# Loading the first branch's four attention arrays at once, two of them into a free tile of the split pool

## The chip, the cores and the metric

The kernel runs on one core of one Trainium2 chip. The metric is the device time of one execution in microseconds (us); lower is better. A core has five engines that run on their own and wait for each other through semaphores: TensorE (PE, matmuls), VectorE (DVE), ScalarE (ACT), GpSimd (POOL) and SyncE (SP). Here SP issues nearly all DMAs, POOL a few. A DMA that SP issues goes through a hardware queue, one that POOL issues through a software queue; both move their packets on the same 16 DMA engines.

## The reference

One decoder layer over 1024 tokens of width 1024, in f32. Two attentions run side by side, their outputs are projected, gated and added, and a feed-forward block follows. What matters here is the end of the mixer:

```python
oa, _ = banded_window_attention(qa, ka, va, A_WINDOW - 1, sinks)      # 16 heads of 64
ya = jnp.einsum('bte,ed->btd', oa.reshape(Bn, T, A_Q_W), w_branch_a)  # 1024 -> 1024
...
ob = jnp.sum(wts[..., None] * o_all, axis=0).astype(u.dtype)          # 8 heads of 64
yb = jnp.einsum('bte,ed->btd', ob.reshape(Bn, T, B_OUT_W), w_branch_b)
merged = jax.nn.sigmoid(ga) * ya + jax.nn.sigmoid(gb) * yb
return jnp.einsum('btd,de->bte', merged, w_o)
```

## The kernel before

Every f32 product is made of three fp32r matmuls (`mac`, L137 to L139): an operand is split into a rounded part `hi` and the rest `lo`, and hi·hi, hi·lo and lo·hi are summed in PSUM. Each operand must therefore be split before use: ACT copies it to `hi` and DVE subtracts to get `lo` (`split`, L117 and L118; for weights L78 and L79 in the class `Weights`).

In the first phase each pair of heads yields one array of attention output, 128x1024 f32 (512 KB). It is scaled and stored to DRAM: eight arrays `oa_d[0..7]` of the window attention, four `ob_d[0..3]` of the dilated one. The last of them, pair 7, is served by POOL instead of SP and DVE (`side`, L618): POOL stores the sums (L610), fetches them back spread over the partitions into the tile `vt` (L615, two DMAs of 256 KB), multiplies them into the tile `o` (L624) and stores `o` to `oa_d[7]` (L625).

The second phase projects them in three branches of four arrays each: branch 0 takes `oa_d[0..3]`, branch 1 `oa_d[4..7]`, branch 2 `ob_d`. A branch has eight steps (`dc`), each 24 matmuls for two PSUM tiles of 128x512. A step with dc = 0 runs with the array `k` as its outer loop: six matmuls for array 0, six for array 1, and so on. Before branch 0, PE multiplies one gate (48 matmuls, L137 to L139 on `u`), which needs none of the arrays.

`o_parts(b)` brings the four arrays of a branch in and splits them, in the order of `k`. `send_parts` issues the loads on SP. It has two raw tiles (`o_raw`, pool `mix`), so at most two arrays are on their way; each of the next two loads waits until a raw tile has been split. The results go into tiles `o_hl` of the pool `low`, six tiles of 8 KB per partition that are handed out in turn. When the second phase starts, the memory of `low` lies where tiles of the first phase were. A tile is free when the last instruction on the old tile in its place is done: the first tile of `low` has nothing to wait for, the second some stores of SP, the third the store of `o` by POOL, the fourth the two fetches into `vt`. SP, ACT, DVE and POOL each work strictly in the order in which the code issues.

The work of SP behind these loads, in order: weights of the branch (`w_raw`, L55), the columns of a modulation matrix (`a_raw`, L822).

Of the kernel before, what the change touches and what calls it, by code (L numbers as in the profile page):

```python
# [10 lines left out]
F32 = mybir.dt.float32  # L11
# [7 lines left out]
P = 128  # L19
T = 1024  # L20
# [78 lines left out]
def decoder_layer(ctx: ExitStack, tc: tile.TileContext, I, out, dbg=None):  # L99
# [685 lines left out]
    mix = ph2b.enter_context(tc.tile_pool(name="mix", bufs=2, reuse_waits="tile"))  # L785
# [7 lines left out]

    o_src = [oa_d[p] for p in range(A_PAIRS)] + [ob_d[p] for p in range(B_PAIRS)]
    o_raws, o_sent = [], [0]

    def send_parts(upto):
        while o_sent[0] < min(upto, len(o_src)) and len(o_raws) < 2:
            raw = mix.tile([P, T], F32, name="o_raw", bufs=2)
            nc.sync.dma_start(raw, o_src[o_sent[0]])  # L800
            o_raws.append(raw)
            o_sent[0] += 1

    def o_parts(b):
        parts = []
        for k in range(4):
            send_parts(4 * b + 4)
            hl = low.tile([P, 2, T], F32R, name="o_hl", tag="big")
            split(hl[:, 0], hl[:, 1], o_raws.pop(0))
            parts.append(hl)  # L810
        return parts
# [61 lines left out]
            nc.gpsimd.tensor_tensor(m, m, tmp, op=OP.add)  # L873

    mg = None
    send_parts(2)

    def split_merged(dcs):
        for dc in dcs:
# [5 lines left out]
    for kind, i in order:  # L885
        if kind == "g":
            if i in (8, 9, 17):
                ws.prepare(4)
                parts = o_parts({8: 0, 9: 1, 17: 2}[i])
                make_gate(i, ())  # L890
            else:
                make_gate(i)
            if i == 23:
                mg = wide("m", bigu)
                split_merged(range(0, 3))
            continue
        b, dc = steps[i]
        w = ws.take(1)
        ps = [ps_2.tile([P, TH], F32, name="p2") for _ in range(2)]
        for n, (t, k) in enumerate([(t, k) for t in range(2) for k in range(4)] if dc not in (0, KC - 1) else  # L900
                                   [(t, k) for k in range(4) for t in range(2)]):
            s = slice(t * TH, (t + 1) * TH)
            mac(ps[t], w(k), (parts[k][:, 0, s], parts[k][:, 1, s]), k == 0, k == 3)
            if n == 3:
                ws.step()
        if dc == 3:
            send_parts(len(o_src))
        for t in range(2):
            merge(b, dc, t, ps[t], gts.get(i))
        next(ada, None)  # L910
        if i == 22:
            split_merged(range(3, 6))
# [500 lines left out]
```

## Time and profile before

| | |
|---|---|
| median of three runs | 1901.1 us (1900.1 to 1901.41) |
| profiled execution, its own time | 1908.77 us |
| span of the profiled execution, first to last instruction | 1907.0 us |
| mean granted TensorE clock | 0.987 of full speed |
| PE busy | 1841.1 us, 97% of the span |
| PE waiting for the splits of branch 0 | 8.0 us in one wait, at 834.3 to 842.3 us |

Times inside the profile are us from the span's start. The profiled execution is 7.7 us longer than the median of the plain runs, and 1.8 us of it lie outside the span. A timeline names at each row the idle time ahead of it and what ended that.

### The profile page before, as it was taken

Reading aid. Unit: us, or ns where it says so; the run is one execution under the profiler, and the core shown is the slowest. Engines: PE = TensorE matmul, PEld = TensorE weight load, DVE = VectorE, ACT = ScalarE, POOL = GpSimd, SP = SyncE. Lnnn points to the kernel's source line nnn. Section 1 sums busy time; section 2 is a strip of 40 time slices with the busy share of each in tenths; the row PEclk is TensorE's granted clock in tenths of the full one; section 3 lists DMA queues with packets and bytes.
Section 4 is the critical chain, followed back from the end, with each engine's and each line's share of the span. In section 5 each row is a group of like instructions: output and inputs, shape, how many; then the busy total and the mean of one; then the engine's idle time right before and its main releaser. Section 6 shows DMA issues by size and latency. Waiting matters only on the chain.

```text
span 1907.0 us, 24471 instructions
## 1 busy us (share of the span) xinstructions
PE 1841.1 (97%) x8988; PEld 1489.6 (78%) x8988; DVE 1160.4 (61%) x2161; ACT 782.0 (41%) x1661; POOL 596.5 (31%) x389
## 2 busy tenths in 40 slices
PE   6899999999999999989999999999999999899998
PEld 5688877878878777768888878778888888788886
DVE  7855667667677887534555364575565444565557
ACT  3455545445444767633122132653333333412122
POOL 2432223223323222100311142455664333431213
PEclk9899999999999999989999999999999999999999
DMA  8011112111121122254534123123222222432222
GB/s 316 28 34 34 40 41 74 45 57 56 41 63 50 53 89 68 79 178 164 175 118 161 56 75 124 56 89 100 89 78 89 78 89 95 135 125 90 93 71 89
DMA packets 72266, 170.83 MB, mean 90 GB/s; under 512 B 13073, under 2 KB 14161, under 8 KB 72146
## 3 DMA queue, kind: packets, MB, share of 16 engines
q1 hardware_dynamic: 71810, 168.21, 26.7%
q8 instruction: 71, 1.16, 0.3%
q0 software_dynamic: 336, 1.06, 0.2%
q14 instruction: 49, 0.40, 0.1%
HBM read 145.80 MB, written 23.43 MB: 89 GB/s over the span
## 4 chain that ended last, share of the span: by engine, by line
PE 51%; DVE 3%; ACT 1%; issue 1%; DMA 1%; SPq 0%; POOL 0%; DVEq 0%; ACTq 0%; POOLq 0%
PE pf L1106 21%; PE p L138 5%; PE p L139 5%; PE p L137 5%; PE pf L137 5%; PE pf L139 5%; PE pf L138 5%; DVE m L118 1%; DMA h_raw<-h_d 0%; DVE wd L79 0%; DVE h L118 0%; DMA oa_d<-o 0%; PE px L1034 0%; PE p L835 0%; PE p L842 0%
## 5 line engine op out<-in xcount | busy, mean ns | idle before, releaser
L137 PE MATMUL pj<-u,w_hi 128*128 128x512 f32 x720 | 301.5, 419 | 0.0
L139 PE MATMUL pj<-u,w_lo 128*128 128x512 f32 x720 | 283.9, 394 | 0.0
L138 PE MATMUL pj<-u,w_hi 128*128 128x512 f32 x720 | 282.6, 392 | 0.0
L425 POOL TENSOR_TENSOR rb<-rb,sin_t 128x512 f32<-128x512 f32 x64 | 86.8, 1356 | 502.0 <-DVE rb L423 431.5
L118 DVE TENSOR_TENSOR w_lo<-r,w_hi 128x512 fp32r<-128x512 f32 x110 | 117.7, 1072 | 138.7 <-ACT w_hi L117 137.9
L79 DVE TENSOR_TENSOR w_lo<-w_raw,w_hi 128x512 fp32r<-128x512 f32 x150 | 133.4, 893 | 85.3 <-ACT w_hi L78 83.0
L528 ACT ACTIVATE probs<-probs,st 128x128 f32<-128x128 f32 (+1 forms) x320 | 146.0, 461 | 60.5 <-DVE st L518 30.8
L137 PEld LDWEIGHTS pj<-u,w_hi 128*128 128x128 f32 x720 | 136.4, 189 | 33.6 <-issue 4.7
L139 PEld LDWEIGHTS pj<-u,w_lo 128*128 128x128 f32 x720 | 135.8, 189 | 30.7
L138 PEld LDWEIGHTS pj<-u,w_hi 128*128 128x128 f32 x720 | 136.7, 190 | 22.6
L137 PE MATMUL pf<-wd,h 128*128 128x512 f32 x352 | 139.2, 395 | 3.4 <-DVE zt L1326 2.9
L138 PE MATMUL pf<-wd,h 128*128 128x512 f32 x352 | 138.7, 394 | 1.9 <-DVE wd L79 1.9
L139 PE MATMUL pf<-wd,h 128*128 128x512 f32 x352 | 138.6, 394 | 0.0
L62 POOL TENSOR_TENSOR w_raw<-w_raw,gate 128x512 f32<-128x512 f32 x60 | 83.1, 1404 | 157.0 <-DMA w_raw<-in_w_down 134.4
L1326 DVE SCALAR_TENSOR_TENSOR zt<-zt,pf 128x512 f32<-128x512 f32 x112 | 76.2, 685 | 85.1 <-PE pf L139 85.0
L426 POOL TENSOR_TENSOR r<-ra,rb 128x512 f32<-128x512 f32 x63 | 114.5, 1817 | 6.1 <-DVE kl L460 1.3
L78 ACT ACTIVATE w_hi<-w_raw 128x512 fp32r<-128x512 f32 x150 | 92.0, 624 | 29.0 <-PE p L138 12.0
L552 ACT ACTIVATE ptsb<-pt 128x512 f32<-128x512 f32 (+1 forms) x128 | 63.6, 548 | 93.6 <-PE pt L550 93.2
L137 PE MATMUL p<-u,w_hi 128*128 128x512 f32 x224 | 88.3, 394 | 0.0
L139 PE MATMUL p<-u,w_lo 128*128 128x512 f32 x224 | 87.2, 389 | 0.0
L138 PE MATMUL p<-u,w_hi 128*128 128x512 f32 x224 | 87.2, 389 | 0.0
L137 PE MATMUL p<-o_hl,w_hi 128*128 128x512 f32 x192 | 75.9, 395 | 8.0 <-ACT o_hl L117 8.0
(297 smaller groups left out, 4267.2 us busy)
## 6 DMA issues: line engine op xcount, KB each, us to landing
w_raw<-in_w_in SPq DMA_DIRECT2D x118, 256.0 KB
r<-in_w_gate_up SPq DMA_DIRECT2D x47, 512.0 KB
a_raw<-in_w_ada SPq DMA_DIRECT2D x32, 512.0 KB
w_raw<-in_w_down SPq DMA_DIRECT2D x44, 256.0 KB
h_raw<-h_d SPq DMA_DIRECT2D x22, 512.0 KB
h_d<-g SPq DMA_DIRECT2D x40, 256.0 KB
wa<-in_w_ada_m SPq DMA_DIRECT2D x16, 512.0 KB
wb<-wt_d SPq DMA_DIRECT2D x24, 256.0 KB
```

The source lines that it names most:

```text
L62: self.nc.gpsimd.tensor_tensor(self.raws[i], self.raws[i], scale(), op=OP.mult)
L78: self.nc.scalar.activation(hi, raw, AF.Copy)
L79: self.nc.vector.tensor_tensor(lo, raw, hi, op=OP.subtract)
L118: nc.vector.tensor_tensor(lo, src, hi, op=OP.subtract)
L137: nc.tensor.matmul(ps, w[0], m[0], start=first, stop=False)
L138: nc.tensor.matmul(ps, w[0], m[1], start=False, stop=False)
L139: nc.tensor.matmul(ps, w[1], m[0], start=False, stop=last)
L425: eng.tensor_tensor(b, b, sin_t[:, s], op=OP.mult)
L426: eng.tensor_tensor(residue_half(res, r, t), by_residue(a, r), by_residue(b, r), op=OP.add)
L528: nc.scalar.activation(pr, pr, AF.Exp, bias=st[:, 0, h, b:b + 1], accum_out=st[:, 1, h, b:b + 1])
L1106: nc.tensor.matmul(ps, w[:, c], m[:, k], start=first and k == 0 and n == 0, stop=k == 3 and n == 2, skip_group_check=True)
L1326: nc.vector.scalar_tensor_tensor(z, z, ALPHA if gi == 0 else 1.0, pd, op0=OP.mult, op1=OP.add)
```

## The change

The loads of branch 0's four arrays are issued together, ahead of the first split. Arrays 0 and 1 go into the two `o_raw` tiles as before. Arrays 2 and 3 go into `raw23`, a new tile with room for both, taken from the pool `low` ahead of the tiles for the splits. From the fifth array on the limit is two again.

```diff
     o_raws, o_sent = [], [0]
+    raw23 = low.tile([P, 2, T], F32, name="raw23", tag="big")
 
     def send_parts(upto):
-        while o_sent[0] < min(upto, len(o_src)) and len(o_raws) < 2:
-            raw = mix.tile([P, T], F32, name="o_raw", bufs=2)
+        while o_sent[0] < min(upto, len(o_src)) and len(o_raws) < (4 if o_sent[0] < 4 else 2):
+            raw = raw23[:, o_sent[0] - 2] if o_sent[0] in (2, 3) else mix.tile([P, T], F32, name="o_raw", bufs=2)
             nc.sync.dma_start(raw, o_src[o_sent[0]])
...
     mg = None
-    send_parts(2)
+    send_parts(4)
```

SP's queue where the second phase starts, before. The names in brackets are the semaphores that an instruction waits for: DMAHW0 to 7 stand for SP's own DMAs in turn, DVE, PE and Pool for those engines.

```order
L700 DMA ga_d_110<-r_7436 128x1024 [waits DMAHW7_49,DVE_49]
L800 DMA o_raw_7689<-oa_d_108 128x1024 [waits DMAHW0_49,PE_49]
L800 DMA o_raw_7691<-oa_d_108 128x1024 [waits DMAHW1_49,Pool_49]
L55 DMA w_raw_7697<-in_w_branch_a 128x512 [waits DVE_49]
L55 DMA w_raw_7703<-in_w_branch_a 128x512 [waits DMAHW3_49,DVE_49]
L800 DMA o_raw_7708<-oa_d_108 128x1024 [waits DMAHW4_49,DMAHW0_49,DVE_49]
L800 DMA o_raw_7713<-oa_d_108 128x1024 [waits DMAHW5_49,DMAHW1_49,DVE_49]
L822 DMA a_raw_7743<-in_w_ada 128x1024 [waits DMAHW6_49,PE_49]
L822 DMA a_raw_7771<-in_w_ada 128x1024 [waits DMAHW7_49]
```

The same place of SP's queue now:

```order
L700 DMA ga_d_110<-r_7436 128x1024 [waits DMAHW7_49,DVE_49]
L801 DMA o_raw_7690<-oa_d_108 128x1024 [waits DMAHW0_49,PE_49]
L801 DMA o_raw_7692<-oa_d_108 128x1024 [waits DMAHW1_49,Pool_49]
L801 DMA raw23_7688<-oa_d_108 128x1024
L801 DMA raw23_7688<-oa_d_108 128x1024 [waits DMAHW3_49]
L55 DMA w_raw_7700<-in_w_branch_a 128x512 [waits DMAHW4_49,DVE_49]
L55 DMA w_raw_7706<-in_w_branch_a 128x512 [waits DMAHW5_49,DVE_49]
L823 DMA a_raw_7742<-in_w_ada 128x1024 [waits DMAHW6_49,PE_49]
L823 DMA a_raw_7770<-in_w_ada 128x1024 [waits DMAHW7_49]
```

The loads of arrays 2 and 3 no longer wait for DVE's splits, stand ahead of the two weight loads, and nothing of the queue behind them waits for a split any more.

ACT's queue at the four splits of branch 0, before. DMASW3 is the semaphore of POOL's store of `o` to `oa_d[7]`, Pool that of POOL's product ahead of it, DMASW1 and DMASW2 those of POOL's two fetches into `vt`.

```order
L78 ACTIVATE w_hi_7699<-w_raw_7470 128x512 [waits DMAHW1_49]
L117 ACTIVATE o_hl_7705<-o_raw_7689 128x1024 [waits DMAHW0_49]
L117 ACTIVATE o_hl_7710<-o_raw_7691 128x1024 [waits DMAHW6_49,DMAHW1_49,DMAHW7_49,DVE_49,Activation_49]
L117 ACTIVATE o_hl_7715<-o_raw_7708 128x1024 [waits DMAHW4_49,DMASW3_49,Pool_49]
L117 ACTIVATE o_hl_7718<-o_raw_7713 128x1024 [waits DMAHW5_49,DMASW2_49,DMASW1_49]
L681 ACTIVATE gt_7721<-p2_7722 128x512 [waits PE_49]
```

The same four splits in ACT's queue now:

```order
L78 ACTIVATE w_hi_7702<-w_raw_7470 128x512 [waits DMAHW1_49]
L117 ACTIVATE o_hl_7708<-o_raw_7690 128x1024 [waits DMAHW6_49,DMAHW0_49,DMAHW7_49,DVE_49,Activation_49]
L117 ACTIVATE o_hl_7711<-o_raw_7692 128x1024 [waits DMAHW1_49,DMASW3_49,Pool_49]
L117 ACTIVATE o_hl_7714<-raw23_7688 128x1024 [waits DMAHW2_49,DMASW2_49,DMASW1_49]
L117 ACTIVATE o_hl_7717<-raw23_7688 128x1024 [waits DMAHW3_49]
L681 ACTIVATE gt_7720<-p2_7721 128x512 [waits PE_49]
```

`raw23` has the first tile of `low`, so each split has the tile after the one that it had: the waits for the old tiles stand one split earlier. The wait for POOL's store, at the third split before, is now at the second. DVE's four subtractions (L118) show the same shift. The order of the matmuls on PE and of all work on POOL is unchanged, and from branch 1 on every split waits as before.

## Rows read from the trace of the kernel before

**Rows 1.** The page's first part: busy time, share of the span and instructions of each engine.

```profile
PE 1841.1 (97%) x8988; PEld 1489.6 (78%) x8988; DVE 1160.4 (61%) x2161; ACT 782.0 (41%) x1661; POOL 596.5 (31%) x389
```

**Rows 2.** The waits of PE over the whole span: us in total, times, longest us.

```profile
PE pt L254 <- DVE acc L242: 11.4, 6, 7.8
PE p L137 <- ACT o_hl L117: 8.0, 1, 8.0
PE s L501 <- DVE qs L440: 7.2, 2, 6.4
```

**Rows 3.** The timeline of PE at the end of the gate and the first step of branch 0: start, us, instruction, and in brackets the idle time before it and what ended it.

```profile
830.58 0.39 PE L139 MATMUL p<-u,w_lo 128*128 128x512 f32 x1
830.80 0.39 PE L137 MATMUL p<-o_hl,w_hi 128*128 128x512 f32 x1
...
832.16 0.39 PE L137 MATMUL p<-o_hl,w_hi 128*128 128x512 f32 x1
832.90 0.50 PE L138 MATMUL p<-o_hl,w_hi 128*128 128x512 f32 x1 [0.35 <-DVE o_hl L118]
...
833.93 0.39 PE L139 MATMUL p<-o_hl,w_lo 128*128 128x512 f32 x1
842.32 0.80 PE L137 MATMUL p<-o_hl,w_hi 128*128 128x512 f32 x1 [8.00 <-ACT o_hl L117]
843.58 0.80 PE L138 MATMUL p<-o_hl,w_hi 128*128 128x512 f32 x1 [0.46 <-DVE o_hl L118]
...
844.60 0.63 PE L137 MATMUL p<-o_hl,w_hi 128*128 128x512 f32 x1
845.03 0.63 PE L138 MATMUL p<-o_hl,w_hi 128*128 128x512 f32 x1
```

**Rows 4.** The timeline of ACT from the first split to the second step of branch 0 and beyond; L866 empties a PSUM tile when its 12 matmuls are done.

```profile
827.82 1.06 ACT L117 ACTIVATE o_hl<-o_raw 128x1024 fp32r<-128x1024 f32 x1 [6.44 <-DMA o_raw<-oa_d]
830.53 1.06 ACT L117 ACTIVATE o_hl<-o_raw 128x1024 fp32r<-128x1024 f32 x1 [1.64 <-DMA o_raw<-oa_d]
841.21 2.00 ACT L117 ACTIVATE o_hl<-o_raw 128x1024 fp32r<-128x1024 f32 x2 [9.62 <-DMA oa_d<-o]
843.12 1.06 ACT L681 ACTIVATE gt<-p 128x512 f32<-128x512 f32 x2
844.08 0.63 ACT L78 ACTIVATE w_hi<-w_raw 128x512 fp32r<-128x512 f32 x1
...
854.08 0.60 ACT L866 ACTIVATE zt<-p 128x512 f32<-128x512 f32 x1 [2.12 <-PE p L139]
...
859.52 0.60 ACT L866 ACTIVATE zt<-p 128x512 f32<-128x512 f32 x1 [2.12 <-PE p L139]
```

**Rows 5.** The timeline of DVE at the same four splits.

```profile
828.92 1.23 DVE L118 TENSOR_TENSOR o_hl<-o_raw,o_hl 128x1024 fp32r<-128x1024 f32 x1 [6.73 <-ACT o_hl L117]
831.62 1.23 DVE L118 TENSOR_TENSOR o_hl<-o_raw,o_hl 128x1024 fp32r<-128x1024 f32 x1 [1.48 <-ACT o_hl L117]
842.30 2.36 DVE L118 TENSOR_TENSOR o_hl<-o_raw,o_hl 128x1024 fp32r<-128x1024 f32 x2 [9.46 <-ACT o_hl L117]
```

**Rows 6.** The timeline of POOL, all that it does between 821 and 904 us.

```profile
821.29 0.68 POOL L610 DMA_DIRECT2D wa_d<-sr  x1 [44.55 <-DVE sr L609]
825.34 1.03 POOL L615 DMA_DIRECT2D vt<-wa_d  x2 [3.36 <-DMA wa_d<-sr]
833.86 2.35 POOL L624 TENSOR_TENSOR o<-o,vt 128x1024 f32<-128x1024 f32 x1 [7.49 <-issue]
836.50 0.60 POOL L625 DMA_DIRECT2D oa_d<-o  x1 [0.30 <-POOL o L624]
```

**Rows 7.** The timeline of SP's DMA issues at the start of the second phase.

```profile
821.25 1.72 SPq L800 DMA_DIRECT2D o_raw<-oa_d  x2
823.02 0.90 SPq L55 DMA_DIRECT2D w_raw<-in_w_branch_a  x2
830.17 3.03 SPq L800 DMA_DIRECT2D o_raw<-oa_d  x2
833.29 0.86 SPq L822 DMA_DIRECT2D a_raw<-in_w_ada  x2
```

**Rows 8.** DMA traffic in two stretches, 826.5 to 833 us and then 831 to 834 us, by queue: packets, MB, share of the 16 engines (q1 is SP's queue, q0 POOL's); and the issues of POOL with the time from issue to landing.

```profile
q1 hardware_dynamic: 468, 1.15, 53.1%
q0 software_dynamic: 160, 0.52, 33.5%
...
q1 hardware_dynamic: 156, 0.57, 71.2%
...
oa_d<-o POOLq DMA_DIRECT2D x1, 512.0 KB, 4.6
```

**Rows 9.** Stretches of the trace: from and to in us, busy time of PE, PEld, DVE, ACT and POOL (instructions), granted TensorE clock, share of the DMA engines, GB/s.

```profile
674.20:677.60 3.40, 3.40 (x10) 2.77 (x10) 3.33 (x8) 1.97 (x5) 0.00 (x0) 0.51 0.64 158
...
826.40:827.80 1.40, 1.40 (x8) 1.17 (x7) 0.00 (x0) 0.00 (x0) 0.00 (x0) 1.00 1.02 389
827.80:830.40 2.60, 2.60 (x13) 2.13 (x13) 1.23 (x1) 1.06 (x1) 0.00 (x0) 1.00 0.97 241
830.40:832.60 2.20, 2.15 (x10) 1.46 (x8) 0.98 (x1) 1.06 (x1) 0.00 (x0) 1.00 0.70 203
...
842.30:848.30 6.00, 5.51 (x12) 4.08 (x13) 5.49 (x7) 3.00 (x5) 0.00 (x0) 0.50 0.08 22
```

## The prediction

> **What bounds the kernel now.** First the busy shares: PE is busy for 97% of the span, and no engine beside TensorE for more than 61% [rows 1]. So a change counts as far as it moves PE's idle time or its clock. Next the waits of PE, longest first: the second longest of all is a single wait of 8.0 us for ACT's split of an array of attention output [rows 2]. That is the place of the change. The timeline of PE shows where it lies: the gate's last matmul starts at 830.58, the six matmuls on array 0 from 830.80, the six on array 1 from 832.16 (with 0.35 us for DVE in between), and then nothing until 842.32, when array 2 is there [rows 3].
>
> Who ends that wait? The loads of arrays 2 and 3 were issued from 830.17, each when a raw tile had been split [rows 7], so it looks as if they came late because of that. The timeline of ACT says otherwise: the third split starts at 841.21, and the idle time before it is ended by the landing of POOL's store of `o` [rows 4]. That store was issued at 836.50 and took 4.6 us [rows 6, 8], which gives 841.1. Array 2 itself was long there: SP's queue moved 0.57 MB between 831 and 834 us, which is the whole of that load and a little more [rows 8]. The third split waits because its `o_hl` tile lies where POOL's `o` lay, as the order of ACT shows. The chain behind this wait is POOL's: sums stored at 821.29, fetched into `vt` from 825.34, product at 833.86 after 7.49 us of waiting for that fetch, store at 836.50 [rows 6].
>
> **What the change does, part by part.**
>
> *The loads.* Arrays 2 and 3 are issued about 7 and 9 us earlier, at about 823 to 825 us, and land before they are needed. By themselves they gain nothing, since the third split did not wait for its load. Arrays 0 and 1 are issued as before and ahead of them in the queue, so the first split starts at about 827.8 again. The two weight loads move back by the time of two issues, 1.7 us [rows 7]; they serve steps that begin after 850 us, and PE's time until then hides that. The two `a_raw` loads, which stood behind the waiting loads until 833.29, follow at about 826 us. Only DVE's sums of the modulation use them, behind the four splits in its queue, so they gain nothing either.
>
> *The wait that moves.* `raw23` takes the first tile of `low`, the one with nothing to wait for. The four splits have the second to fifth tile. The first split now waits for stores that SP issued before 821.25, ahead of its own load in the same queue: nothing. The second split now has the tile under POOL's `o`, and waits for the same store at 841.1 that the third waited for. So PE has the six matmuls of array 0 at 830.8, stops at 832.2 instead of 834.3, and resumes when the second split's first half is done, 1.06 us after the store lands [rows 4]: at 842.3 if the store is no later. The wait grows from 8.0 to about 10.1 us. Behind the second split on ACT stand the other two splits, the gate's two activations and the next weight split; they ran from 841.21 to 844.7 [rows 4] and take 1.0 us more with one more split ahead of them. On DVE it is 1.2 us more [rows 5]. The weights so delayed serve the third step, after 854 us, so nobody waits for that.
>
> *The price of it.* Before the change 12 of the step's 24 matmuls were left at 842.3, now 18. The six more cost, at full clock, a quarter of a step: successive steps end 5.44 us apart (854.08 to 859.52 [rows 4]), so **1.36 us**. At the lower clock, where matmuls start 0.43 us apart (844.60 to 845.03 [rows 3]), they would cost 2.6 us. I take 1.36, because what is at the lower clock is a stretch of time: PE resumes at 842.32 and runs at 0.50 of its clock until 848.3 [rows 9], and the six matmuls push the rest of the work to behind 848.3, where it runs at full clock. The other three splits cost nothing more: they follow each other on ACT at 1.0 us, and six matmuls take 1.4 us or more.
>
> *The store that may come later.* POOL's fetch into `vt` shares the DMA engines with SP's loads. Before, SP had little queued from about 828 to 831; now arrays 2 and 3 (1.05 MB), the weights and the `a_raw` loads (1.05 MB) stand there at once. No row shows the two queues full at the same time, so I bound the delay. From below: in the fetch's own stretch, 827.8 to 832.6, the engines moved 2.6 us at 241 and 2.2 us at 203 GB/s [rows 9], 1.07 MB, of which the fetch was 0.52 [rows 8]: it already shared about evenly. With even shares again it lands when it did, and the store might gain some tenths, since the `a_raw` loads that ran beside it are over: -0.3 us. From above: all of SP's loads go first. The traffic before, from 826.4 to 832.6, was 1.62 MB, some 0.35 of it from array 2; now 1.27 + 2.1 = 3.37 MB must move. With 0.52 MB at the fetch's pace (2.4 us at about 220 GB/s) and 2.85 MB at the 389 GB/s that SP's loads reached at 826.4 to 827.8 [rows 9] (7.3 us), that ends at 836.1 instead of 832.6: +3.5 us. I take **+1.0 us**, nearer to the even sharing, because that is what the one stretch with both queues shows, but not at it, since SP's queue now never runs dry.
>
> The Trainium skill (DMA: Bandwidth & Descriptors, Queues, rings and completion order) says that a DMA engine takes turns between the queues that have work, and changes only after a whole packet of descriptors. By that rule the fetch would wait for one packet of SP's at each turn and no longer, and the sum below would be near +1.4 rather than +2.4; the even shares in [rows 9] agree with it, and no row tests it with SP's queue full throughout.
>
> *The clock.* PE's stretch at 0.50 after the pause cost 3.0 us of full-clock work (half of 842.3 to 848.3 [rows 9]). The pause is now longer, but it was already long enough to lose the clock. Its end may come one short stretch earlier or later; the shortest low stretch here is 3.4 us, 674.2 to 677.6 [rows 9], worth 1.7 us. I take 0, and keep 1.7 both ways for the range.
>
> **The sum.** 1.36 + 1.0 = +2.4 us. The profiled execution was 1908.77 us with a span of 1907.0; after, about 1911.2 and 1909.4. It lies 7.7 us above the median of the plain runs; I carry the difference over to the median: 1901.1 + 2.4 = **1903.5 us**. PE works without a long break behind this place, so what it loses here it does not get back.
>
> **The rivals.**
>
> *The fetch is pushed far back (slower).* The same shift of the wait, but SP's loads go ahead of POOL's fetch nearly all the way: +1.36 + 3.5 = +4.9, 1906.0 us. It decides from a fetch that is 2.5 us later on, where the sum passes 3.8 us. For it: SP's queue holds 2.1 MB more in that stretch. Against it: the even sharing above, and that most of this traffic also ran before the fetch ended in the profile of before, array 2 beginning at 831.
>
> *The late loads were the cause (faster).* If the third split had waited for its load and POOL's store only landed at the same moment, the loads at once would end the stop: -8.0 us, and -3.0 us for the clock that is then not lost, 1890.1. For it: the loads did stand behind splits. Against it: the landing of array 2 by 834 [rows 8], and the wait for the store in ACT's order, which now stands at the second split.
>
> *Nothing changes.* The change doesn't do what it says to PE: the six matmuls fall into a stretch where something else holds PE up anyway, such as an earlier end of the low clock, 1901.1. For it: the sum is small. Against it: from 848.3 on PE runs without a gap that could hide it.
>
> **How the numbers follow.** Forecast 0.70; pushed-back fetch 0.20; late loads 0.04; nothing 0.06. A difference of 0.2% (3.8 us) is about what a measurement of this kernel can tell from no change, so the forecast at +2.4 and the case of no change count as the same, but for a tail of the forecast, 0.04, in which the delay and the clock both come out badly. That gives slower 0.20 + 0.04 = 0.24, same 0.66 + 0.06 = 0.72, faster 0.04. The range: down to no delay of the fetch and the clock back early, 1901.1 + 1.36 - 0.3 - 1.7 = 1900.5; up to the pushed-back fetch, 1906.0, and a little for the clock, 1906.4. This leaves out the late loads and the tails.
>
> **What would show it.** In the profile after: SP issues four loads in a row from 821.25 and the weights at about 825; ACT starts the first split at 827.8 and the other three in a row at about 842; PE's wait for ACT's split is about 10 to 11 us and begins at 832.2, after six matmuls and not twelve; POOL's product starts between 833.6 and 837.4, likely near 834.9. PE then runs some 6 us at half clock. I am wrong if the second split starts before POOL's store has landed, if the first split is late too, or if PE's wait is under 8 us.

## The result and the profile after

| | before | after |
|---|---|---|
| median of 20 runs of each | 1900.88 us (1899.09 to 1902.91) | 1903.53 us (1901.72 to 1905.84) |
| ratio after/before | | 1.0015 (95%: 1.0009 to 1.0021) |
| profiled execution | 1908.77 us | 1905.39 us |
| PE's wait for the splits of branch 0 | 8.0 us | 10.3 us |

The change makes the kernel 2.65 us slower by the medians (1.7 to 4.0 us by the interval of the ratio). That is 0.15%, clear of no change, and under the 0.2% that the prediction counted as a difference. The forecast was 1903.5.

Single profiles do not show that: the profiled execution of after is the shorter one. The profile of before held low-clock stretches far from this place, such as 674.2 to 677.6 us [rows 9], and its mean granted clock is 0.987, that of after 0.990. So the sum is made on the medians, and the place is read by itself. There, too, two traces are offset: TensorE's last transpose ahead of POOL's chain (L607) starts at 819.77 in before and at 818.06 in after. I call that start t0; "t0 + 7.18" is 7.18 us behind it, and all comparisons below are made so. Line numbers shift by one or two where an edit adds lines (L866 is L867 in after), and the profile leaves digits out of names, so `raw23` is `raw` there.

The waits of PE in after (us in total, times, longest):

```profile
PE pt L254 <- DVE acc L242: 11.9, 6, 7.1
PE p L137 <- ACT o_hl L117: 10.3, 1, 10.3
PE s L501 <- DVE qs L440: 7.2, 2, 6.4
```

The list is that of [rows 2], and one entry has moved by more than half a microsecond: 8.0 is now 10.3. PE's timeline in after, from the transpose at t0 to where it resumes:

```profile
818.06 0.27 PE L607 MATMUL pt<-ident,es 128*16 128x128 f32 x1
...
830.23 0.39 PE L139 MATMUL p<-o_hl,w_lo 128*128 128x512 f32 x1
840.95 0.80 PE L137 MATMUL p<-o_hl,w_hi 128*128 128x512 f32 x1 [10.34 <-ACT o_hl L117]
842.21 0.79 PE L138 MATMUL p<-o_hl,w_hi 128*128 128x512 f32 x1 [0.47 <-DVE o_hl L118]
```

PE stops after 830.6, at t0 + 12.6, when it has had the six matmuls of array 0. Before it stopped at t0 + 14.6, after twelve [rows 3]. It resumes at t0 + 22.89 (before t0 + 22.55). ACT's timeline says on what:

```profile
824.40 1.06 ACT L117 ACTIVATE o_hl<-o_raw 128x1024 fp32r<-128x1024 f32 x1 [4.72 <-DMA o_raw<-oa_d]
839.85 1.06 ACT L117 ACTIVATE o_hl<-o_raw 128x1024 fp32r<-128x1024 f32 x1 [14.38 <-DMA oa_d<-o]
840.81 1.99 ACT L117 ACTIVATE o_hl<-raw 128x1024 fp32r<-128x1024 f32 x2
...
848.28 1.28 ACT L867 ACTIVATE zt<-p 128x512 f32<-128x512 f32 x2 [3.99 <-PE p L139]
851.68 0.60 ACT L867 ACTIVATE zt<-p 128x512 f32<-128x512 f32 x1 [1.60 <-PE p L139]
854.40 0.60 ACT L867 ACTIVATE zt<-p 128x512 f32<-128x512 f32 x1 [2.12 <-PE p L139]
```

The second split, which reads a raw tile that landed long ago, waits 14.38 us for the landing of POOL's store `oa_d<-o`, as the third did before [rows 4]. The other two follow in a row. The fourth PSUM tile of the branch (the second half of the second step) is emptied at t0 + 36.34; before it was t0 + 34.31. POOL's timeline in after shows the chain behind the store:

```profile
819.59 0.68 POOL L610 DMA_DIRECT2D wa_d<-sr  x1 [44.55 <-DVE sr L609]
825.24 1.03 POOL L615 DMA_DIRECT2D vt<-wa_d  x2 [4.97 <-DMA wa_d<-sr]
834.19 2.33 POOL L624 TENSOR_TENSOR o<-o,vt 128x1024 f32<-128x1024 f32 x1 [7.92 <-issue]
836.82 0.60 POOL L625 DMA_DIRECT2D oa_d<-o  x1 [0.30 <-POOL o L624]
```

From t0 the fetch is issued at 7.18 (before 5.57), the product starts at 16.13 (14.09), the store is issued at 18.76 (16.73) [rows 6]. The DMA issues of POOL in after, with us from issue to landing:

```profile
oa_d<-o POOLq DMA_DIRECT2D x1, 512.0 KB, 3.0
vt<-wa_d POOLq DMA_DIRECT2D x2, 256.0 KB, 7.5
wa_d<-sr POOLq DMA_DIRECT2D x1, 8.0 KB, 5.1
```

The store is 2.03 us late, but lands in 3.0 us instead of 4.6 [rows 8], with nothing of SP's beside it any more: SP's queue moved 0.76 MB between 836.5 and 841.2 us in before and nothing between 836.82 and 839.85 us in after. So the second split is released at t0 + 21.79, only 0.35 us behind the third split of before. SP's issues in after are the four loads, the weights and the modulation's columns in one run:

```profile
819.54 1.42 SPq L801 DMA_DIRECT2D o_raw<-oa_d  x2
821.01 0.99 SPq L801 DMA_DIRECT2D raw<-oa_d  x2
822.10 0.96 SPq L55 DMA_DIRECT2D w_raw<-in_w_branch_a  x2
823.16 1.45 SPq L823 DMA_DIRECT2D a_raw<-in_w_ada  x2
```

All of them are issued when POOL's fetch is (825.24); before, half of them came after it [rows 7]. Two stretches of after: from the fetch's issue to the product, and PE's low clock once it resumes (columns as in [rows 9]):

```profile
825.24:834.19 8.95, 5.38 (x24) 4.13 (x22) 1.23 (x1) 0.22 (x1) 1.03 (x2) 0.99 1.03 332
...
840.95:847.70 6.75, 6.28 (x14) 4.62 (x15) 6.61 (x8) 3.33 (x5) 0.00 (x0) 0.50 0.04 5
```

The DMA engines are full over the 8.95 us from the fetch's issue to the product (share 1.03). PE runs 6.75 us at half clock after the pause (6.0 before [rows 9]).

### The profile page after: what moved, and what is told of

Read it like the earlier page. It is cut to its first block, busy times and chain, and to the rows that moved or that the text cites. A ratio compares the mean times of both kernels' runs of the same rounds, so it can differ in the third digit from the quotient of the medians.

```text
span 1903.6 us, 24471 instructions
## 1 busy us (share of the span) xinstructions
PE 1835.7 (96%) x8988; PEld 1484.8 (78%) x8988; DVE 1162.5 (61%) x2161; ACT 781.8 (41%) x1661; POOL 597.5 (31%) x389
## 5 line engine op out<-in xcount | busy, mean ns | idle before, releaser
L118 DVE TENSOR_TENSOR w_lo<-r,w_hi 128x512 fp32r<-128x512 f32 x110 | 117.7, 1073 | 138.7 <-ACT w_hi L117 136.6
L137 PE MATMUL p<-o_hl,w_hi 128*128 128x512 f32 x192 | 76.1, 396 | 10.3 <-ACT o_hl L117 10.3
```

The source lines that it names most:

```text
L118: nc.vector.tensor_tensor(lo, src, hi, op=OP.subtract)
L137: nc.tensor.matmul(ps, w[0], m[0], start=first, stop=False)
```

## The experiments

The theory on record for the first runs was the prediction's own: the wait for the old tile stands six matmuls earlier, and POOL's chain is a little later. The rival was that the loads at once are what costs, since they crowd POOL's fetch. Each run below is timed in turn with the kernel before on the same chip; a difference is that of the two medians (11 runs of each edited kernel that was timed, but 9 of e4_store_elsewhere and 5 of e7_act_fetch). Times at the place are counted from t0.

**More profiles of both kernels.** One profile of before and one of after may not stand for their kernels, so three more executions were profiled, without a change: `e9_before_look1` and `e10_before_look2` (before), `e11_after_look` (after).

> The kernel before once more, for a second profile of the place. Theory: the medians of all runs so far lie 0.6 to 2.2 us above what their profiles give against the one profile of before, so that profile was about 1.3 us slow at this place; counted from the last transpose of the sums, the second step's second half was emptied at 34.3 us there, and near 33 us it is typical. Rival: 34.3 again, and the medians hold something that the place doesn't show.

> The same again, a third profile of the kernel before: near 33 us by the theory, 34.3 us by the rival; POOL's fetch takes 5 to 8.5 us from issue to product, its store 4 to 5 us.

> The changed kernel once more, for a second profile of the place. Theory: as in the first, 9 us from the fetch's issue to the product, 3 us for the store, the second step's second half emptied at 36.3 us from the last transpose of the sums, plus or minus 0.5. Rival (the place varies from run to run by as much as the change costs): outside of that by over 1 us.

They took 1901.08, 1900.58 and 1902.09 us, one execution each. The fourth PSUM tile was emptied at t0 + 32.34 and 31.72 in the two of before, on the theory's side of 34.3 and below its 33, and at 35.32 in e11_after_look, a miss: 1.0 us under the 36.3 expected, and more than the 0.5 allowed. In e10_before_look2 the store took 3.30 us, not 4 to 5. POOL's timeline in e9_before_look1, whose t0 is 816.48:

```profile
818.01 0.68 POOL L610 DMA_DIRECT2D wa_d<-sr  x1 [44.56 <-DVE sr L609]
823.29 1.03 POOL L615 DMA_DIRECT2D vt<-wa_d  x2 [4.61 <-DMA wa_d<-sr]
828.94 2.36 POOL L624 TENSOR_TENSOR o<-o,vt 128x1024 f32<-128x1024 f32 x1 [4.61 <-issue]
831.60 0.60 POOL L625 DMA_DIRECT2D oa_d<-o  x1 [0.30 <-POOL o L624]
```

Here the fetch takes 5.65 us from issue to product, not the 8.52 of the first profile of before [rows 6], and the product starts at t0 + 12.46. So the profile on which the prediction rests had one of before's late fetches. What the fetch had beside it, in e9_before_look1 (823.29 to 828.94) by queue: packets, MB, share of the 16 engines:

```profile
q1 hardware_dynamic: 421, 1.07, 59.9%
q0 software_dynamic: 160, 0.52, 36.2%
```

and in after (825.24 to 834.19):

```profile
q1 hardware_dynamic: 818, 2.45, 79.9%
q0 software_dynamic: 160, 0.52, 23.2%
```

The same 0.52 MB goes beside 1.07 MB of SP's in the one and beside 2.45 MB in the other. These stretches run from issue to product and hide two parts. In after, first without a packet of the fetch (825.24 to 828.74), then while it moves (828.74 to 832.74):

```profile
q1 hardware_dynamic: 504, 1.44, 102.6%
...
q1 hardware_dynamic: 198, 0.59, 55.5%
q0 software_dynamic: 147, 0.52, 50.8%
```

and in before, the two stretches of [rows 9] that the prediction read (827.8 to 830.4, then 830.4 to 832.6):

```profile
q0 software_dynamic: 139, 0.48, 78.1%
q1 hardware_dynamic: 86, 0.15, 19.1%
...
q1 hardware_dynamic: 103, 0.40, 63.5%
q0 software_dynamic: 20, 0.05, 6.5%
```

So in before the fetch moved first, nearly alone, and SP's array 2 after it; the two did not share. In after they do, at about half the engines each, and the fetch's first packets also come later. All twelve runs in which POOL fetches (those below included) fall into these two kinds. With all loads at once the fetch's third packet moves 3.2 to 4.1 us after the issue, and from there until 0.50 MB are moved it takes 3.2 to 4.0 us with 52 to 62% of the engines. With two loads at a time it is 1.3 to 2.9 us, and then 2.0 to 3.0 us with 67 to 91%.

All profiles of the two kernels together:

| counted from t0, us | fetch issued | product starts | store issued | split released | fourth PSUM tile emptied |
|---|---|---|---|---|---|
| before | 5.57 | 14.09 | 16.73 | 21.44 | 34.31 |
| e9_before_look1 | 6.81 | 12.46 | 15.12 | 19.60 | 32.34 |
| e10_before_look2 | 5.52 | 12.88 | 15.54 | 18.84 | 31.72 |
| after | 7.18 | 16.13 | 18.76 | 21.79 | 36.34 |
| e11_after_look | 7.65 | 16.51 | 19.14 | 22.17 | 35.32 |

By the means, the product starts 3.2 us later (13.14 to 16.32), the store takes 1.1 us less (4.16 to 3.03 from issue to release), and so the split is released 2.0 us later (19.96 to 21.98). The fourth tile is 3.0 us later (32.79 to 35.83), near the +2.65 of the medians. Of the product's 3.2 us, 1.4 us are the fetch's later issue (5.97 to 7.42) and 1.7 us its longer time from issue to product (7.18 to 8.91).

**The loads alone.** `e1_loads_only` issues four loads at once, but arrays 2 and 3 go into memory that is not of the pool `low`, so that each split keeps the tile that it had.

```diff
-        while o_sent[0] < min(upto, len(o_src)) and len(o_raws) < 2:
-            raw = mix.tile([P, T], F32, name="o_raw", bufs=2)
+        while o_sent[0] < min(upto, len(o_src)) and len(o_raws) < (4 if o_sent[0] < 4 else 2):
+            raw = merged[1][:, o_sent[0]] if o_sent[0] in (2, 3) else mix.tile([P, T], F32, name="o_raw", bufs=2)
...
-    send_parts(2)
+    send_parts(4)
```

> All four loads of branch 0 at once, but arrays 2 and 3 go into the half of the second accumulator (merged[1]) that is not written before the fifth step, so that the splits keep the tiles they had before the change. Theory (the moved wait is what costs, the loads only change when POOL's store lands): the third split still waits for POOL's store, PE stops at 834.3 as before, the store lands 0 to 0.5 us later, time +0.3 us against the kernel before (1.0000 to 1.0004). Rival (the crowd of loads on the DMA engines is what costs): the full +2.6 us of the change, ratio 1.0014.

Measured: 1903.96 us against 1901.33, ratio 1.0012 (1.0003 to 1.0020), +2.6 us. The theory's +0.3 us lies just below the interval and the rival's +2.6 in it: with no wait moved, the loads alone cost about as much as the whole change. The fourth tile is emptied at t0 + 35.33, 2.5 us behind the mean of before. The wait is for the third split, as before, and POOL's product starts at t0 + 16.36, with the fetch issued at 6.88. One limit of this run: the memory used for arrays 2 and 3 comes free late, so their loads are issued at t0 + 6.41 and the weights behind them at 7.29, not at 2.95 and 4.04 as in after. Even so the fetch takes 9.48 us.

**The shift alone.** `e2_shift_only` takes the first tile of `low` for raw tiles, so that the splits move on by one tile, but still loads two arrays at a time.

```diff
+    raw01 = low.tile([P, 2, T], F32, name="raw01", tag="big")
...
-            raw = mix.tile([P, T], F32, name="o_raw", bufs=2)
+            raw = raw01[:, o_sent[0] % 2] if o_sent[0] < 4 else mix.tile([P, T], F32, name="o_raw", bufs=2)
```

> The first tile of the split pool is taken by the raw tile, as in the change, but the loads stay two at a time: arrays 0 and 2 share one half, 1 and 3 the other. Theory: the second split waits for POOL's store, PE stops after six matmuls, and six matmuls more are left behind the pause: +1.4 us against before, up to +2.4 because the fourth load can now start only when the second split is done at about 843.5, so that its split comes late by up to 1 us. Rival (the loads are what costs): 0.

Measured: 1902.08 us, ratio 1.0002 (0.9993 to 1.0011), +0.75 us: inconclusive, since 0 and +1.4 both lie within the interval. Its ACT timeline (t0 is 818.65):

```profile
836.86 2.00 ACT L117 ACTIVATE o_hl<-raw 128x1024 fp32r<-128x1024 f32 x2 [10.14 <-DMA oa_d<-o]
842.85 1.06 ACT L117 ACTIVATE o_hl<-raw 128x1024 fp32r<-128x1024 f32 x1 [3.99 <-DMA raw<-oa_d]
```

The wait for the store did move (one split stands before it, not two), but the release came at t0 + 18.21, as early as in before's best profile. The second raw tile is read only after that wait, so the fourth load, and SP's `a_raw` loads behind it, could not start until then: POOL's fetch took only 4.98 us and its store 3.0. So this run also removed traffic, and is no clean measure of the shift.

**The shift by two.** `e3_shift_two` puts arrays 0 and 1 into two tiles of `low`, so that the first split gets the tile under POOL's `o`.

```diff
-            raw = mix.tile([P, T], F32, name="o_raw", bufs=2)
+            raw = low.tile([P, 2, T], F32, name="raw01", tag="big")[:, 0] if o_sent[0] < 2 else mix.tile([P, T], F32, name="o_raw", bufs=2)
...
-    send_parts(2)
+    send_parts(4)
```

The limit of the loop is four for the first four arrays, as in e1_loads_only.

> The loads at once as in the change, but arrays 0 and 1 are loaded into two tiles of the split pool and 2 and 3 into the two old raw tiles: the splits have the third to sixth tile, and the very first split waits for POOL's store. Theory: PE stops before the first of the step's 24 matmuls, another six are behind the pause: 1.4 us above the changed kernel, +4.0 us against before (1.0021). Rival (the loads are what costs, the place of the wait doesn't matter): the same as the change, +2.6 us.

Measured: 1906.01 us, ratio 1.0024 (1.0015 to 1.0033), +4.7 us, for +4.0 expected. ACT's first split in e3_shift_two, whose t0 is 817.66:

```profile
839.30 2.00 ACT L117 ACTIVATE o_hl<-raw 128x1024 fp32r<-128x1024 f32 x2 [20.02 <-DMA oa_d<-o]
```

It waits 20.02 us for the same store. The release is at t0 + 21.64, within 0.6 us of after's 21.79 and 22.17, so it is not a later store that puts this run above the change. The differences of the medians are 2.0 us apart (+4.7 and +2.65), the fourth tile is 1.35 us later than the mean of after. Over all runs in which the store ends the wait, the time from the release to the fourth emptied tile is as below. The last column takes off what PE lost to the low clock in that time, half of the stretch at 0.50, which lasted 3.6 to 7.1 us in these runs:

| the split that waits | us from the release to the fourth tile, each profile | mean | less the low clock |
|---|---|---|---|
| third (before, e9, e10, e1, and e6 below) | 12.87, 12.74, 12.88, 13.31, 12.75 | 12.9 | 9.93, 9.83, 9.82, 9.77, 9.84 |
| second (after, e11, and e5 below) | 14.55, 13.15, 14.41 | 14.0 | 11.19, 11.34, 11.22 |
| second, with the fourth load late (e2) | 15.27 | | 12.01 |
| first (e3) | 15.54 | 15.5 | 12.65 |

Without the low clock each split that the wait moves ahead costs 1.4 us, twice; the sum had 1.36. e2_shift_only stands by itself, as its last split waited another 3.99 us for its load.

**The wait taken away.** `e4_store_elsewhere` lets POOL write its product into the free tile `wb` and store that. The store then no longer holds the memory of `o`, only the product does, since it reads `o`. The loads are as before.

```diff
+        d = att.tile([P, T], F32, name="wb", bufs=1) if p == A_PAIRS - 1 else o
-        side(p)[1].tensor_tensor(o, o, sums.pop(p), op=OP.mult)
-        side(p)[0].dma_start(oa_d[p], o)
+        side(p)[1].tensor_tensor(d, o, sums.pop(p), op=OP.mult)
+        side(p)[0].dma_start(oa_d[p], d)
```

> The kernel before, but POOL's product for pair 7 goes into another tile (wb) and is stored from there, so that the memory of the old tile o is free when the product ends (836.2) and not when its store lands (841.1). Theory: the third split starts at 836.2, PE resumes near 837.3 instead of 842.3: -5.0 us, and up to -3.0 us more if the shorter pause of 3 us keeps TensorE at its higher clock: -5 to -8 us, ratio 0.9974 to 0.9958. Rival (arrays 2 and 3 came late because their loads were issued late): the third split moves little, 0 to -1 us.

Measured: 1895.74 us, ratio 0.9972 (0.9962 to 0.9983), -5.6 us. It is faster than both kernels. The third and fourth split on ACT in e4_store_elsewhere, whose t0 is 818.22:

```profile
833.66 1.06 ACT L117 ACTIVATE o_hl<-o_raw 128x1024 fp32r<-128x1024 f32 x1 [5.45 <-POOL wb L625]
835.51 1.06 ACT L117 ACTIVATE o_hl<-o_raw 128x1024 fp32r<-128x1024 f32 x1 [0.80 <-DMA o_raw<-oa_d]
```

The third split waits for the product, at t0 + 15.44, and not for the store; PE's wait falls to 2.7 us. The loads still stand behind the splits, and only at the fourth split does the load come last, by 0.80 us. So late loads were not the cause of the stop.

**The loads at once without the wait for the store.** `e12_after_store_elsewhere` makes e4's edit on the kernel after.

> The changed kernel with POOL's product stored from another tile: the second split is released by the end of the product and not by the landing of the store. Theory (price of the change = six matmuls behind the pause, 1.4 us, plus a fetch that ends 3 us later beside the loads): 4.4 us above the kernel before with the same edit (e4, -5.6 us), that is -1.2 us against before, with the clock between -1.5 and +0.5. Rival (the six matmuls alone): 1.4 us above it, -4.2 us against before.

Measured: 1898.98 us against 1901.04, ratio 0.9988 (0.9979 to 0.9997), -2.1 us. The theory (-1.2, 4.4 us above e4_store_elsewhere) and the rival (-4.2, 1.4 above) differ in the distance to e4. It is 3.5 us by the two differences (3.2 by the medians as they stand), nearer to the theory, but the two intervals are 1.7 and 2 us wide to each side, so the times alone do not rule the rival out. The place does. POOL's product and the split that waits for it, the second, in e12_after_store_elsewhere (t0 817.18):

```profile
831.92 2.33 POOL L625 TENSOR_TENSOR wb<-o,vt 128x1024 f32<-128x1024 f32 x1 [8.18 <-DMA w_raw<-in_w_branch_a]
...
834.29 1.06 ACT L117 ACTIVATE o_hl<-o_raw 128x1024 fp32r<-128x1024 f32 x1 [9.31 <-POOL wb L625]
```

The product starts at t0 + 14.74, the release is at 17.11, 1.7 us behind e4's, where the rival has nothing; with 1.36 for the six matmuls that makes 3.0 us.

**The fetch by ACT's queue.** `e7_act_fetch` has e4's edit, and lets ACT issue the store of pair 7's sums and the fetch into `vt`. `e8_act_fetch_loads` is e7 with the four loads at once, as in e1.

```diff
-        side(p)[0].dma_start(wa_d[p].rearrange("h (b q) -> (h b) q", q=P), sr[:16])
+        (nc.scalar if p == A_PAIRS - 1 else nc.sync).dma_start(wa_d[p].rearrange("h (b q) -> (h b) q", q=P), sr[:16])
...
-            side(key)[0].dma_start(wb[h * 64:(h + 1) * 64], src[h:h + 1].to_broadcast([64, T]))
+            (nc.scalar if key == A_PAIRS - 1 else nc.sync).dma_start(wb[h * 64:(h + 1) * 64], src[h:h + 1].to_broadcast([64, T]))
```

> The kernel with POOL's product stored from another tile, and the sums of pair 7 stored and fetched by ACT's queue instead of POOL's; loads two at a time as before. Theory: the product ends before the third split is due, so what is left of PE's stop is the wait for the loads of arrays 2 and 3, 1 to 2.5 us, without loss of clock: -9 to -10.5 us against before, -3.5 to -5 us against the run with the store elsewhere. Rival (POOL's chain no longer matters once its store is out of the way): as that run, -5.5 us.

> The same with all four loads at once (arrays 2 and 3 into the unused half of the second accumulator). Theory: with the wait for POOL gone the loads are what PE's stop is left for, so now loading at once gains what the run before still loses: PE doesn't stop, -11 to -12 us against before, 1 to 2.5 us below the run with two at a time. Rival (loads at once always lose to the crowd on the DMA engines): the same as that run or up to 2.6 us above it.

Measured: e7_act_fetch 1894.41 us against 1901.64, ratio 0.9962 (0.9950 to 0.9975), -7.2 us, less than expected, and the lowest median of all versions. The rival's -5.5 lies in the interval, so by the time alone e7 is not told from e4. e8_act_fetch_loads 1898.58 us, ratio 0.9987 (0.9979 to 0.9996), -3.1 us: its expectation fell. With nothing but the loads between them, two at a time is 4.2 us better than four at once. ACT's timeline in e7_act_fetch, t0 817.77:

```profile
823.35 1.13 ACTq L615 DMA_DIRECT2D vt<-wa_d  x2
...
831.90 1.06 ACT L117 ACTIVATE o_hl<-o_raw 128x1024 fp32r<-128x1024 f32 x1 [4.33 <-DMA o_raw<-oa_d]
```

and in e8_act_fetch_loads, t0 817.97 (`zt` is the accumulator's name):

```profile
823.14 1.14 ACTq L615 DMA_DIRECT2D vt<-wa_d  x2
...
834.52 2.00 ACT L117 ACTIVATE o_hl<-zt 128x1024 fp32r<-128x1024 f32 x2 [7.14 <-POOL wb L625]
```

In e7 the third split waits for its load, and only here do the late loads end PE's stop, which is 1.3 us long. The theory had no loss of clock, and that failed (columns as in [rows 9]):

```profile
835.20:838.60 3.40, 3.40 (x10) 2.65 (x9) 2.55 (x6) 1.09 (x3) 0.00 (x0) 0.51 0.61 245
```

Half of these 3.40 us, 1.7, is about what -7.2 lacks to the -9 expected at least. In e8 that load is early, but the split now waits for POOL's product. The product starts 9.00 us after the fetch's issue (5.17 to 14.17 from t0) and not 5.44 (5.58 to 11.02). The loads at once take away one wait and lengthen the one beside it by more.

**Part of the traffic taken away.** `e5_after_late_a` and `e6_before_late_a` hold the `a_raw` loads back, until after the gate, on after and on before:

```diff
-            if n % 4 == 2:
+            if n % 4 == 2 and i != 8:
                 next(ada, None)
```

> The changed kernel, but the first two a_raw loads (1.05 MB, modulation matrix) are issued some 20 us later, behind the gate, so that they are not queued beside POOL's fetch and store. Theory (the second part of the price is the crowd of SP's loads beside POOL's fetch, which took 9.0 us from issue to product in the profiles with all loads at once and 5.0 to 8.5 with two at a time): fetch to product 6 to 7 us, the second split released some 2 us earlier: 2 us below the change, about +0.5 us against before (0.9995 to 1.0008). Rival (the six matmuls behind the pause are the whole price): +2.6 us as the change itself.

> The kernel before with the same edit: the first two a_raw loads behind the gate. In the profile of before they ran beside POOL's store of o, which took 4.6 us; without them it took 3.0 us in the other profiles. Theory: the third split is released 1.6 us earlier, -1 to -1.6 us against before. Rival: the store's time has nothing to do with these loads, 0.

Measured: e5_after_late_a 1903.98 us against 1901.64, ratio 1.0013 (1.0003 to 1.0023), so nothing gained over after. e6_before_late_a 1901.74, ratio 1.0002 (0.9993 to 1.0011), no gain either. Both expectations missed. In e5 the fetch still takes 8.20 us (t0 + 7.23 to 15.43), and its third packet comes 3.2 us after the issue, with the loads of the four arrays and the weights alone beside it: these are enough to hold it back. Once it moves it has 62% of the engines and SP 28%, and still needs 3.5 us for 0.50 MB, so the shares are not all of it. The split is released at 21.09, 0.9 us sooner than in after by the means, not 2. In e6 the store lands sooner (3.04 us from issue to release) as expected, but the fetch took 8.68 us, though nothing had been added.

## Why the prediction was right

*The bound, and the place of the wait.* Right, and shown. The store ends the third split's wait before and the second's after, by ACT's rows in both. e4_store_elsewhere takes the store out of the wait and gains 5.6 us with the loads untouched.

*The loads by themselves gain nothing.* Right as to the gain: in e1_loads_only and e8_act_fetch_loads they cost. SP's four loads stand in a row from t0 + 1.48 as forecast. ACT's first split starts at t0 + 6.34, where 8.05 was said, but the two other profiles of before have 6.13 and 6.48. The weights were issued at t0 + 4.04, 0.8 us later than before and not 1.7, as the second pair of issues took 0.99 us and not the 1.72 of the first pair in [rows 7].

*Six more matmuls behind the pause, 1.36 us.* Right. Measured as 1.4 us for each of two splits, from nine profiles, once the low clock is taken off. As they stand single profiles do not show it to better than a microsecond (13.15 to 14.55 among three), because the stretch at half clock is of another length in each.

*The store that may come later, +1.0 us.* That it comes later was right, and this is the term that was mis-sized. Over five profiles the release is 2.0 us later, as a sum of two: the product 3.2 us later, the store 1.1 us shorter. The step that failed is the reading of even shares in [rows 9]. The 0.52 and 0.55 MB moved there one after the other, the fetch with 78.1% of the engines before the loads of arrays 2 and 3 were under way. Even shares are not what the fetch had before but what it got in after, where its 0.52 MB took 4.0 us to move; before, 0.48 MB took 2.6. The 3.5 us ahead of its first packets in after (2.5 before) had no term at all. Nor had the fetch's later issue (1.4 of the 3.2 us), which follows from a later landing of the 8 KB store. That part is not shown to come from the loads: the fetch is issued at t0 + 5.53 to 7.65 in the runs with all loads at once, and at 5.41 to 7.57 in those with two at a time. The store's gain was "some tenths", and was 1.1 us. All this was judged from one profile of before, in which fetch and store were slow already (8.52 and 4.71 us); two more have 5.65 and 7.36, 4.48 and 3.30. In the first pair of profiles alone the release is 0.35 us later, which would have looked like a confirmation of a smaller term.

That the loads at once delay the fetch is shown by more than these: the product starts between t0 + 14.74 and 16.51 in all six runs with POOL's fetch and four loads at once (after, e11, e1, e3, e5, e12), and between 12.46 and 14.09 in all six with two at a time (before, e9, e10, e2, e4, e6). With ACT's fetch it is 14.17 (e8) against 11.02 (e7).

The prediction weighed a rule of the Trainium skill (DMA: Bandwidth & Descriptors, Queues, rings and completion order), that an engine takes turns between the queues that have work, and derived that the fetch would hardly be delayed. The trace agrees with the rule where both queues move packets, and not with what was derived: in 828.74 to 832.74 of after the fetch has 147 packets and 50.8% of the engines, SP 198 and 55.5%. Turns with a queue that never runs dry leave the fetch half of the engines, where before it had most of them. From the fetch's issue at 825.24 to 828.74 SP's queue moved 504 packets and the fetch's none, and no run shows why.

*The clock, 0.* Right within the 1.7 us that it allowed: after the pause the clock was at 0.50 for 5.8 to 6.1 us in the three profiles of before, and for 6.75 us in after, but 3.6 us in e11_after_look. By the means that is 0.4 us of full-clock work less.

*The rivals.* "Late loads were the cause" is refuted by e4 and e8. "Nothing changes" is refuted by the ratio's interval. "The fetch is pushed far back" came near in the product (3.2 us of its 3.5 later), but not by SP going ahead all the way: once the fetch moves it has its half, and part of the 3.2 us is its later issue. The shorter store gives a third of it back, so that the sum does not pass 3.8 us.

*The sum.* 1.4 for the six matmuls and 2.0 for the release make 3.4 us by the means of all profiles; with the 0.4 us that the clock gave back the two kernels' own fourth tiles are 3.0 us apart. The medians are 2.65 apart (1.7 to 4.0). So +2.4 was within what the runs can tell, but that it came within 0.3 us is in part luck: its second term was half of the measured one, and itself a difference of two that were both too small. How much of the change is the shift and how much the loads, the medians of e1 (+2.6) and e2 (+0.75) do not settle, since either edit also changed when the other loads ran; e1 and after have nearly the same median, though after has the six matmuls more behind its wait.

*What stays open.* What holds the fetch's first packets back for 3.2 to 4.1 us: SP's queue has the engines full in that time, but the loads were not tried one by one. Why the fetch then moves slowly in e5 too, where SP has little left to move. Whether the loads also delay the 8 KB store. Why e6 gained nothing: in three of six runs with two loads at a time the fetch took 7.4 to 8.7 us, and in all three its issue was early (t0 + 5.41 to 5.57, against 6.81 to 7.57 in the others). In two of them, before and e6, 0.50 MB had moved 5.5 to 5.7 us after the issue, and the last few packets came beside SP's array 2 over the next two; what makes it so was not tested.

## What to carry to other kernels

Before loading earlier, look at what ends the wait: here it was not the load but the landing of a store from the memory that the next tile lies in, and changing that store's place gave 5.6 us where the earlier loads with the moved wait cost 2.65. A "free" tile taken from a pool that is handed out in turn moves every later tile by one place, so ask which old user each of them then waits for, and how much work is left behind that wait. Loads issued early into a quiet queue are not free when another transfer is the one that ends the chain: here it kept half of the engines, not most of them, and began later; and a term of a microsecond wants several profiles of before, since one had a fetch 2.9 us longer than another of the same kernel.

## What the runs showed of the hardware

- A 512 KB fetch spread over the partitions took 5.0 to 8.7 us to POOL's product with SP's loads two at a time, and 8.2 to 9.5 us with them at once. On ACT's hardware queue it was 5.44 and 9.00 us, so it is not a matter of POOL's software queue.
- Two queues that both had packets shared the engines about evenly: 50.8% for the fetch and 55.5% for SP's loads in 828.74 to 832.74 us of after. But the fetch's first packets moved only 3.2 to 4.1 us after the issue where SP's queue held all loads, and 1.3 to 2.9 us with two at a time.
- The same 512 KB store took 3.0 us from issue to the release where SP's loads were over or held back, in after, e11, e1, e2, e3, e5 and e6, and 3.3 to 4.7 us in the three profiles of before, with `a_raw` loads beside it.
- An 8 KB store kept POOL idle for 3.2 to 5.5 us until it landed, without the order of the code around it having changed: 3.36, 4.61 and 3.31 us in three profiles of before.
